# A differential-attention layer on one Trainium2 core: scores by products over 64 rows, three a map, in place of products over 128 rows, four a pair

## The chip, the core and the metric

The kernel runs on one core of one Trainium2 chip. Five engines work side by side, each on its own list of instructions in a fixed order: TensorE (PE) multiplies, VectorE (DVE), ScalarE (ACT) and GpSimd (POOL) do elementwise work, and SyncE (SP) issues the DMAs. They wait for one another through semaphores. TensorE reads its operands from SBUF and writes into eight banks of PSUM; the weights of a product are loaded by an operation of their own, which the profile lists as PEld. The metric is the device time of one execution in microseconds.

## The reference

One layer takes 2048 latent tokens and 128 context tokens of width 1024 through a normalisation, one input projection (queries, keys, values and the three inputs of a short convolution), attention beside convolution, an output projection, and a feed-forward block. The part that matters here is the attention. Each of the four heads has two maps with queries and keys of 64 numbers each; the two softmaxes are subtracted with a learned weight before they meet the values:

```python
s = jnp.einsum('bqhmd,bkhmd->bhmqk', qblk.astype(jnp.float32), kf) * ATTN_SCALE
p = jax.nn.softmax(s, axis=-1)
a = p[:, :, 0] - lam * p[:, :, 1]
return jnp.einsum('bhqk,bkhe->bqhe', a, vf)
```

Latent queries read 2176 keys (2048 latent and 128 cached ones), context queries their own 128. All is held to float32 accuracy.

## The kernel before

**Numbers in two parts.** TensorE takes its operands in a float32 form that it rounds (F32R). So `split` (lines 79 to 82) writes every operand as a rounded part and a remainder: ScalarE copies (L81), VectorE subtracts (L82). A product of two such numbers is then three products: high by high, high by low, low by high.

**Stages.** From 0 to 408 us the input projection and the split queries, keys and values are made. Queries and keys are turned by `stack` (L241) and go to DRAM (`qd`, `kd`, `kpd`). From 408 to about 1370 us lies the attention stage, to 1554 the rest of the output projection, and behind it the feed-forward block, first `psg` (L956 to L959), then `psy` (L1085 to L1087).

**Scores before.** A head vector has 64 numbers, and TensorE has 128 rows to sum over. The kernel lays the high part of a map's key in rows 0 to 63 and its low part in rows 64 to 127, one tile `km[m]` a map. The query tile `qt` has the high part of the query twice, once in each half of the rows, and the low part twice. Two products over 128 rows then give all four combinations, high and low query with the whole key, the fourth (low by low) without being asked for. A block of 128 queries against 2176 keys is done in five pieces of 436 or 432 columns (`KC`), each into one of three PSUM banks (`pss`, tile `s`):

```python
for s in range(2):
    mm = T.matmul(ps[:, :n], qt[:, s, m, t * P:(t + 1) * P], km[m][:, k0:k0 + n], start=(s == 0), stop=(s == 1))
```

VectorE takes each piece out of its bank into `e` with the running maximum (L505). After five pieces it reduces the maxima to `nm` (L509), ScalarE takes the exponential with its sum (L510), and after the second map VectorE forms the weights `r` and `wt` (L513 to L516). GpSimd (L519, L520) and VectorE (L521) share the addition of the second map to the first.

**Values and the filler.** The values of one piece of work (`values`, L526) are computed behind the scores of the next: transposes of `e` on TensorE (L546), a split into `ath` and `atl`, and three products with the values (L537 to L539). Between the scores TensorE gets products of the convolution's inputs (L617 to L619) and, later, of the output projection (L724 to L726). After each eviction `pump` (L781) adds a fixed credit of columns and issues such products, ordered behind the last score product that is in the list `marks`.

**What sets the order.** A scheduler places each engine's instructions when the program is built, by priorities, buffers that come free, and its own estimate of time. On the chip the order of each engine is fixed. The five `e` buffers and one more, the three score banks and the lists on SP are the resources around the change.

Of the kernel before, what the change touches and what calls it, by code (L numbers as in the profile page):

```python
# [8 lines left out]
F32 = mybir.dt.float32  # L9
F32R = mybir.dt.float32r  # L10
BF16 = mybir.dt.bfloat16
AF = mybir.ActivationFunctionType
ALU = mybir.AluOpType
AX = mybir.AxisListType
# [3 lines left out]
P = 128  # L18
# [5 lines left out]
NH = 4  # L24
# [3 lines left out]
SCALE = 0.125  # L28
# [12 lines left out]
def layer(ctx, tc, x_prompt, x_sample, cache_k, cache_v, cond, w_ada, b_ada, gcol,  # L41
# [3 lines left out]
    V, S, G, T = nc.vector, nc.scalar, nc.gpsimd, nc.tensor  # L45

    const = ctx.enter_context(tc.tile_pool(name="const", bufs=1))
    dram = ctx.enter_context(tc.tile_pool(name="dram", bufs=1, space=DRAM))
# [3 lines left out]
    identr = const.tile([P, P], F32R, name="identr")  # L52
# [7 lines left out]
    ud = [dram.tile([2, P, KT, 256], F32, name=f"ud{i}") for i in range(9)]  # L60
    kd = [dram.tile([NH, 2, P, w], F32, name=f"kd{w}") for w in (1792, 384)]
    kpd = dram.tile([NH, 2, P, P], F32, name="kpd")
    qd = [dram.tile([NH, 2, 64, 2, 256], F32, name=f"qd{i}") for i in range(9)]
    vd = dram.tile([18, P, NH, 256], F32, name="vd")
    mixh = [dram.tile([NH, 2, P, 256], F32, name=f"mixh{i}") for i in range(9)]
    mixc = dram.tile([4, 2, P, NALL], F32, name="mixc")
# [3 lines left out]
    def dma(out, in_):  # L70

        out, in_ = (x.bitcast(F32) if x.dtype == F32R else x for x in (out, in_))
        with tc.issue_after(behind[0]) if behind else ExitStack():
            return nc.sync.dma_start(out, in_).ins
# [4 lines left out]
    def split(h, l, src, eng=None):  # L79

        S.copy(h, src)  # L81
        (eng or V).tensor_tensor(l, src, h.bitcast(F32), op=ALU.subtract)  # L82
# [20 lines left out]
    def pool(name, **kw):  # L103
        st = ExitStack()
        return st, st.enter_context(tc.tile_pool(name=name, reuse_waits="tile", **{"bufs": 1, **kw}))
# [135 lines left out]
    def stack(st_list, dst, flip):  # L241

        n = len(st_list)
        for a in range(4):
            tp = psk.tile([P, 512], F32, tag="psk", name="tp")
            tv = tp.rearrange("p (m t) -> p m t", m=2)
            for m in range(2):
                for i, st in enumerate(st_list):
                    T.transpose(tp.bitcast(F32R)[:, m * 256 + i * P:m * 256 + (i + 1) * P],
                                st[:, 2 * a + m, :], identr)  # L250
            o = p1b.tile([P, 2, 256], F32R, tag="sto", name="sto", bufs=2)
            if a % 2 == flip:
                S.copy(o[:, :, :n * P], tv[:, :, :n * P])
            else:
                V.tensor_copy(o[:, :, :n * P], tv[:, :, :n * P])
            dst(a, o, n * P)

    def heads_split(src):

        st = p1b.tile([P, 8, P], F32R, tag="st", name="st", bufs=3)  # L260
        sv = src.rearrange("p (m d) -> p m d", m=8)
        split(st[:, :, 0:64], st[:, :, 64:128], sv)
        return st

    def v_split(src, kt):
# [10 lines left out]

    def q_store(i):
        def f(a, o, n):
            for s in range(2):
                dma(qd[i][a, s, :, :, :n], o[s * 64:(s + 1) * 64, :, :n])  # L280
        return f

    def kp_store(a, o, n):
# [17 lines left out]
    def qkv_out(pq, gi, i, j, rt, sts):  # L301
        if gi == 8 and j > 0:
            so = p1b.tile([P, 512], F32, tag="t1", name="so", bufs=2)
            V.tensor_copy(so, pq)
            dma(state_k if j == 1 else state_v, so)
        if j == 2:
            v_split(pq, 2 * gi + i if gi < 8 else 17)
        else:
            sts.append(heads_split(pq if gi == 8 else rotated(pq, rt, i)))
# [33 lines left out]
    x_pb, p1b = pool("p1b", side="left")  # L343
# [39 lines left out]
    def cached():  # L383
        ck = p1b.tile([P, 512], F32, tag="t1", name="ck", bufs=2)
        dma(ck, cache_k)
        stack([heads_split(ck)], k_store(NLAT), 0)
        cv = p1b.tile([P, 512], F32, tag="t1", name="cv", bufs=2)
        dma(cv, cache_v)
        v_split(cv, 16)
# [11 lines left out]
        bcx_weights(0)  # L401

    def load_q(h, i, w):
        qt = pk.tile([P, 2, 2, 256], F32R, tag="qt", name="qt", bufs=2)
        src = qd[i][h, :, :, :, :w].rearrange("s d m t -> d s m t")
        for s in range(2):
            for r in range(2):
                dma(qt[r * 64:(r + 1) * 64, s, :, :w], src[:, s])
        return qt

    def load_keys(h):
        km = []
        for m in range(2):
            kt_ = pk.tile([P, NALL], F32R, tag="km", name="km", bufs=3)
            dma(kt_[:, :1792], kd[0][h, m])
            dma(kt_[:, 1792:], kd[1][h, m])
            km.append(kt_)
        kp = pk.tile([P, 2, P], F32R, tag="kp", name="kp")
        dma(kp, kpd[h].rearrange("m p t -> p m t"))
        return km, kp  # L420

    wb = {}
# [49 lines left out]
    x_pa, pa = pool("pa", side="left")  # L472
    x_fu, pf = pool("pfu", side="right")
    x_pss, pss = pool("pss", space=PSUM, bufs=3, side="left")
# [6 lines left out]
    def e_tile():  # L481

        ecount[0] += 1
        if x_fu is not None and ecount[0] % 6 == 0:
            return pf.tile([P, NALL], F32, tag="e", name="e")
        return pa.tile([P, NALL], F32, tag="e", name="e", bufs=5)

    def softmaxes(qt, nq, km, kcs):

        nk = sum(n for _, n in kcs)  # L490
        sm = pa.tile([P, 2, 2], F32, tag="sm", name="sm", bufs=3)
        r = pa.tile([P, 2, 2], F32, tag="r", name="r", bufs=3)
        out = []
        for t in range(nq):
            e = []
            for m in range(2):
                et = e_tile()
                mx = pa.tile([P, 5], F32, tag="mx", name="mx", bufs=4)
                for ci, (k0, n) in enumerate(kcs):
                    ps = pss.tile([P, 512], F32, tag="s", name="s")  # L500
                    for s in range(2):
                        mm = T.matmul(ps[:, :n], qt[:, s, m, t * P:(t + 1) * P], km[m][:, k0:k0 + n],  # L502
                                      start=(s == 0), stop=(s == 1))
                        marks.append(mm.ins)
                    V.tensor_scalar(et[:, k0:k0 + n], ps[:, :n], SCALE, None, op0=ALU.mult, op1=ALU.max,  # L505
                                    accum_out=mx[:, ci:ci + 1])
                    pump()
                nm = pa.tile([P, 1], F32, tag="nm", name="nm", bufs=4)
                V.tensor_reduce(nm, mx[:, :len(kcs)], axis=AX.X, op=ALU.max, negate=True)  # L509
                S.activation(et[:, :nk], et[:, :nk], AF.Exp, bias=nm, scale=1.0, accum_out=sm[:, t, m:m + 1])  # L510
                e.append(et)

            V.reciprocal(r[:, t, :], sm[:, t, :])  # L513
            wt = pa.tile([P, 1], F32, tag="wt", name="wt", bufs=3)
            V.tensor_scalar(wt, r[:, t, 1:2], neglam, sm[:, t, 0:1], op0=ALU.mult, op1=ALU.mult)
            V.tensor_scalar(wt, wt, 1e30, -1e30, op0=ALU.min, op1=ALU.max)  # L516
            cut = nk - (POOLW if nk > 128 else 0)
            if cut < nk:
                G.tensor_scalar(e[1][:, cut:nk], e[1][:, cut:nk], wt, 1.0, op0=ALU.mult, op1=ALU.mult)  # L519
                G.tensor_tensor(e[0][:, cut:nk], e[0][:, cut:nk], e[1][:, cut:nk], op=ALU.add)  # L520
            V.scalar_tensor_tensor(e[0][:, :cut], e[1][:, :cut], wt, e[0][:, :cut],  # L521
                                   op0=ALU.mult, op1=ALU.add)
            out.append(e[0])
        return out, r
# [256 lines left out]
    def pump():  # L781

        nonlocal credit
        credit += RATE[x_fu is None]
        while credit > 0:
            with tc.issue_after(marks[-1]) if marks else ExitStack():
                c = next(todo)
            if not c:
                credit = 0.0
                break  # L790
            credit -= c
# [4 lines left out]
    marks = []  # L796
    for n, (h, i) in enumerate(work):
        if i == 0:
            qt = hb.pop("q") if n == 0 else load_q(h, 0, 256)
            km, kp = hb.pop("k") if n == 0 else load_keys(h)  # L800
            vts = load_values(h)
        lat = i < 8
        if i > 0:
            qt = load_q(h, i, 256 if lat else 128)
        if lat:
            ar = softmaxes(qt, 2, km, KC)
        else:
            ar = softmaxes(qt, 1, [kp[:, 0, :], kp[:, 1, :]], ((0, 128),))
        if pending:
            values(*pending)  # L810
        pending = (h, i, ar, vts if lat else vts[17:], 17 if lat else 1)
        ready = max(0, n - 28)
# [71 lines left out]
    start = done  # L884
# [182 lines left out]
    for gn, (c, g) in enumerate(groups):  # L1067
        tiles = seqs[c][3 * g:3 * g + 3]
        w = len(tiles) * P
# [88 lines left out]
```

## Time and profile before

| What | Value |
|---|---|
| Median of three runs | 3085.41 us (3083.14 to 3085.58) |
| The profiled execution | 3085.89 us, span 3084.1 us |
| TensorE busy, over the span | 2914.8 us (95%), granted clock 0.984 |
| VectorE, ScalarE, GpSimd busy | 2082.6 us, 1348.7 us, 1242.9 us |
| Attention stage, 408 to 1370 us: TensorE, VectorE, ScalarE, GpSimd busy | 918.44, 756.61, 571.44, 475.31 us of 962 |
| Score products (L502) and their evictions (L505) | 1296 and 648 |

A busy time is the union of an engine's records. Matmul records overlap: a record lasts longer than the distance to the next start, so the cost of a product is read from the starts in the timeline.

### The profile page before, as it was taken

Reading aid. Unit: us, or ns where it says so; the run is one execution under the profiler, and the core shown is the slowest. Engines: PE = TensorE matmul, PEld = TensorE weight load, DVE = VectorE, ACT = ScalarE, POOL = GpSimd, SP = SyncE. Lnnn points to the kernel's source line nnn. Section 1 sums busy time; section 2 is a strip of 40 time slices with the busy share of each in tenths; the row PEclk is TensorE's granted clock in tenths of the full one; section 3 lists DMA queues with packets and bytes.
Section 4 is the critical chain, followed back from the end, with each engine's and each line's share of the span. In section 5 each row is a group of like instructions: output and inputs, shape, how many; then the busy total and the mean of one; then the engine's idle time right before and its main releaser. Section 6 shows DMA issues by size and latency. Waiting matters only on the chain.

```text
span 3084.1 us, 47310 instructions
## 1 busy us (share of the span) xinstructions
PE 2914.8 (95%) x16921; PEld 2653.6 (86%) x16921; DVE 2082.6 (68%) x4158; ACT 1348.7 (44%) x2383; POOL 1242.9 (40%) x1114
## 2 busy tenths in 40 slices
PE   4899989999999999999999989999999999999998
PEld 3778879998999999988888888999999998788886
DVE  7999568787788887764477775776665554554443
ACT  3323236666565665653344433333333333444432
POOL 7313135554545544532256654554544540111110
PEclk8999999999999999999999999999999999999999
DMA  7777564453454444457645465444632325766663
GB/s 249 249 246 246 171 196 123 136 183 113 136 166 127 139 150 132 119 164 223 183 136 156 150 195 193 145 148 134 238 137 97 102 99 193 239 223 219 219 216 120
DMA packets 351180, 525.25 MB, mean 170 GB/s; under 512 B 33089, under 2 KB 264673, under 8 KB 349153
## 3 DMA queue, kind: packets, MB, share of 16 engines
q1 hardware_dynamic: 350944, 522.23, 52.8%
q8 instruction: 133, 2.18, 0.3%
q14 instruction: 103, 0.84, 0.1%
HBM read 393.79 MB, written 128.34 MB: 169 GB/s over the span
## 4 chain that ended last, share of the span: by engine, by line
PE 65%; DVE 12%; DMA 9%; issue 7%; POOL 4%; ACT 2%; SPq 1%; POOLq 0%; DVEq 0%; ACTq 0%
PE psg L956 6%; PE s L502 6%; PE psg L959 6%; PE psg L957 6%; PE psy L1087 4%; PE psy L1086 4%; PE psy L1085 4%; PE t L546 3%; DVE wi L82 3%; DMA raw<-in_w_fi 2%; PE pq L239 2%; POOL st L918 2%; PE psx L725 2%; PE psx L726 2%; PE psx L724 2%
## 5 line engine op out<-in xcount | busy, mean ns | idle before, releaser
L956 PE MATMUL psg<-u,wi 128*128 128x384 f32 (+1 forms) x1848 | 615.6, 334 | 47.2 <-ACT wi L81 21.1
L957 PE MATMUL psg<-u,wi 128*128 128x384 f32 (+1 forms) x1848 | 606.1, 328 | 0.0
L959 PE MATMUL psg<-u,wi 128*128 128x384 f32 (+1 forms) x1848 | 590.6, 330 | 6.0 <-DVE wi L82 6.0
L505 DVE TENSOR_SCALAR_CACHE_REDUCE e<-s 128x436 f32<-128x436 f32 (+2 forms) x648 | 373.8, 600 | 90.0 <-PE s L502 73.4
L956 PEld LDWEIGHTS psg<-u,wi 128*128 128x128 f32 x1848 | 350.0, 189 | 65.7 <-ACT wi L81 29.6
L502 PE MATMUL s<-km,qt 128*128 128x436 f32 (+1 forms) x1280 | 345.7, 374 | 12.1 <-DVE e L505 9.1
L959 PEld LDWEIGHTS psg<-u,wi 128*128 128x128 f32 x1848 | 347.7, 190 | 10.8 <-DVE wi L82 10.3
L957 PEld LDWEIGHTS psg<-u,wi 128*128 128x128 f32 x1848 | 350.4, 190 | 0.1
L82 DVE TENSOR_TENSOR wo<-rawo,wo 128x1024 fp32r<-128x1024 f32 x132 | 167.0, 1265 | 248.4 <-ACT wo L81 243.7
L82 DVE TENSOR_TENSOR wi<-st,wi 128x512 fp32r<-128x512 f32 x264 | 235.2, 895 | 127.6 <-ACT wi L81 126.1
L510 ACT ACTIVATE e<-e,nm 128x2176 f32<-128x2176 f32 (+1 forms) x136 | 274.0, 2015 | 78.4 <-DVE nm L509 77.7
L81 ACT CAST wi<-st 128x512 fp32r<-128x512 f32 x264 | 163.0, 620 | 323.8 <-POOL st L918 166.2
L1087 PE MATMUL psy<-wo,hhl 128*128 128x512 f32 x748 | 285.8, 391 | 1.8 <-DVE hhl L82 1.8
L1086 PE MATMUL psy<-wo,hhl 128*128 128x512 f32 x748 | 286.3, 390 | 0.9 <-DVE wo L82 0.9
L1085 PE MATMUL psy<-wo,hhl 128*128 128x512 f32 x748 | 285.8, 390 | 0.0
L81 ACT CAST wo<-rawo 128x1024 fp32r<-128x1024 f32 x132 | 139.2, 1054 | 296.2 <-PE psy L1087 286.4
L502 PEld LDWEIGHTS s<-km,qt 128*128 128x128 f32 x1280 | 211.0, 192 | 24.4 <-DVE e L505 15.9
L82 DVE TENSOR_TENSOR atl<-t,ath 128x512 fp32r<-128x512 f32 (+2 forms) x292 | 187.1, 650 | 34.7 <-ACT ath L81 33.9
L81 ACT CAST ath<-t 128x512 fp32r<-128x512 f32 (+2 forms) x292 | 157.2, 554 | 116.2 <-PE t L546 107.6
L918 POOL TENSOR_TENSOR st<-raw,st 128x512 f32<-128x512 f32 x66 | 103.0, 1561 | 231.1 <-DVE wi L82 231.1
L1058 POOL TENSOR_TENSOR rr<-rr,mhalf 128x1 f32<-128x1 f32 x17 | 13.1, 779 | 450.4 <-DVE rr L1057 450.4
L82 DVE TENSOR_TENSOR wi<-raw,wi 128x512 fp32r<-128x512 f32 x198 | 176.6, 892 | 15.7 <-ACT wi L81 15.7
(264 smaller groups left out, 7092.6 us busy)
## 6 DMA issues: line engine op xcount, KB each, us to landing
raw<-in_w_fi SPq DMA_DIRECT2D x132, 512.0 KB, 4.1
rawo<-in_w_fo SPq DMA_DIRECT2D x132, 512.0 KB, 3.4
fu<-ud SPq DMA_DIRECT2D x256, 256.0 KB, 4.7
raw<-in_w_ada SPq DMA_DIRECT2D x48, 512.0 KB, 5.3
u2d<-hl SPq DMA_DIRECT2D x42, 512.0 KB, 3.7
u<-u2d SPq DMA_DIRECT2D x14, 1536.0 KB, 9.4
hr<-hid SPq DMA_DIRECT2D x110, 192.0 KB, 3.5
hid<-hid SPq DMA_DIRECT2D x88, 192.0 KB, 2.1
```

The source lines that it names most:

```text
L81: S.copy(h, src)
L82: (eng or V).tensor_tensor(l, src, h.bitcast(F32), op=ALU.subtract)
L502: mm = T.matmul(ps[:, :n], qt[:, s, m, t * P:(t + 1) * P], km[m][:, k0:k0 + n], start=(s == 0), stop=(s == 1))
L505: V.tensor_scalar(et[:, k0:k0 + n], ps[:, :n], SCALE, None, op0=ALU.mult, op1=ALU.max, accum_out=mx[:, ci:ci + 1])
L510: S.activation(et[:, :nk], et[:, :nk], AF.Exp, bias=nm, scale=1.0, accum_out=sm[:, t, m:m + 1])
L918: G.tensor_tensor(t, x, y, op=op)
L956: T.matmul(ps[:, :n], h[:, ks], u[:, 0, kt, :n], start=start and kt == 0, stop=False, skip_group_check=not start)
L957: T.matmul(ps[:, :n], h[:, ks], u[:, 1, kt, :n], start=False, stop=False, skip_group_check=not start)
L959: T.matmul(ps[:, :n], l[:, ks], u[:, 0, kt, :n], start=False, stop=stop and kt == 3, skip_group_check=not start)
L1085: T.matmul(banks[i][:, b, :], hh, woh_[:, bs], start=(f == 0), stop=False)
L1086: T.matmul(banks[i][:, b, :], hh, wol_[:, bs], start=False, stop=False)
L1087: T.matmul(banks[i][:, b, :], hl, woh_[:, bs], start=False, stop=(f == NF - 1))
```

## The change

Queries and keys are laid out by part instead of by map. A head's vector of 128 numbers now holds map 0 in rows 0 to 63 and map 1 in rows 64 to 127; `km[0]` and the first half of `qt` are the high parts of both maps, `km[1]` and the second half the low parts. `heads_split` and `stack` write this layout, with the same number of transposes and copies. A query tile is stored by one DMA instead of two and loaded by one instead of four, without copies of itself. The scores of a piece for the two maps are written into two banks by six products over 64 rows, three a map, written in the source in turn: map 0, map 1, map 0 and so on. The product of the two low parts is left out. The maxima and exponentials of both maps follow after the pieces of both, and both `e` tiles are taken ahead of the first piece. The three banks, the five pieces and the credit of `pump` are unchanged.

```diff
-    qd = [dram.tile([NH, 2, 64, 2, 256], F32, name=f"qd{i}") for i in range(9)]
+    qd = [dram.tile([NH, P, 2, 256], F32, name=f"qd{i}") for i in range(9)]
@@ stack
-            for m in range(2):
+            for s in range(2):
                 for i, st in enumerate(st_list):
-                    T.transpose(tp.bitcast(F32R)[:, m * 256 + i * P:m * 256 + (i + 1) * P],
-                                st[:, 2 * a + m, :], identr)
+                    T.transpose(tp.bitcast(F32R)[:, s * 256 + i * P:s * 256 + (i + 1) * P],
+                                st[:, a, s, :], identr)
@@ heads_split
-        st = p1b.tile([P, 8, P], F32R, tag="st", name="st", bufs=3)
-        sv = src.rearrange("p (m d) -> p m d", m=8)
-        split(st[:, :, 0:64], st[:, :, 64:128], sv)
+        st = p1b.tile([P, NH, 2, P], F32R, tag="st", name="st", bufs=3)
+        sv = src.rearrange("p (h d) -> p h d", h=NH)
+        split(st[:, :, 0, :], st[:, :, 1, :], sv)
@@ q_store
-            for s in range(2):
-                dma(qd[i][a, s, :, :, :n], o[s * 64:(s + 1) * 64, :, :n])
+            dma(qd[i][a, :, :, :n], o[:, :, :n])
@@ load_q
-        qt = pk.tile([P, 2, 2, 256], F32R, tag="qt", name="qt", bufs=2)
-        src = qd[i][h, :, :, :, :w].rearrange("s d m t -> d s m t")
-        for s in range(2):
-            for r in range(2):
-                dma(qt[r * 64:(r + 1) * 64, s, :, :w], src[:, s])
+        qt = pk.tile([P, 2, 512], F32R, tag="qt", name="qt", bufs=2)
+        dma(qt[:, :, :w], qd[i][h, :, :, :w])
@@ softmaxes
-            e = []
-            for m in range(2):
-                et = e_tile()
-                mx = pa.tile([P, 5], F32, tag="mx", name="mx", bufs=4)
-                for ci, (k0, n) in enumerate(kcs):
-                    ps = pss.tile([P, 512], F32, tag="s", name="s")
-                    for s in range(2):
-                        mm = T.matmul(ps[:, :n], qt[:, s, m, t * P:(t + 1) * P], km[m][:, k0:k0 + n],
-                                      start=(s == 0), stop=(s == 1))
-                        marks.append(mm.ins)
-                    V.tensor_scalar(et[:, k0:k0 + n], ps[:, :n], SCALE, None, op0=ALU.mult, op1=ALU.max,
-                                    accum_out=mx[:, ci:ci + 1])
-                    pump()
+            e = [e_tile() for m in range(2)]
+            mx = [pa.tile([P, 5], F32, tag="mx", name="mx", bufs=4) for m in range(2)]
+            for ci, (k0, n) in enumerate(kcs):
+                ps = [pss.tile([P, 512], F32, tag="s", name="s") for m in range(2)]
+                for x, (sq, sk) in enumerate(((0, 0), (0, 1), (1, 0))):
+                    for m in range(2):
+                        ms = slice(64 * m, 64 * m + 64)
+                        mm = T.matmul(ps[m][:, :n], qt[ms, sq, t * P:(t + 1) * P], km[sk][ms, k0:k0 + n],
+                                      start=(x == 0), stop=(x == 2))
+                        marks.append(mm.ins)
+                for m in range(2):
+                    V.tensor_scalar(e[m][:, k0:k0 + n], ps[m][:, :n], SCALE, None, op0=ALU.mult, op1=ALU.max,
+                                    accum_out=mx[m][:, ci:ci + 1])
+                    pump()
+            for m in range(2):
                 nm = pa.tile([P, 1], F32, tag="nm", name="nm", bufs=4)
...
```

The scheduler places the new products itself, and what it makes of the order in the source can be listed.

TensorE's list before, in the attention stage: `s` is a score bank, `km` the keys of one map, `fb` and `fc` banks of the filler, `o` the values' bank, `t` a transpose.

```order
L539 MATMUL o_5410<-atl_5490,vv_3739 128x256
L502 MATMUL s_5386<-km_3500,qt_5212 128x436 x2
L617 MATMUL fb_5381<-fu_4835,bh_3525 128x256
L618 MATMUL fb_5381<-fu_4836,bh_3525 128x256
L619 MATMUL fb_5381<-fu_4835,bl_3526 128x256
L617 MATMUL fb_5381<-fu_4835,bh_3525 128x256
L618 MATMUL fb_5381<-fu_4836,bh_3525 128x256
L619 MATMUL fb_5381<-fu_4835,bl_3526 128x256
L502 MATMUL s_5396<-km_3500,qt_5212 128x432 x2
```

The same list in the changed program, at the like place: `km_3462` holds the high parts of both maps' keys, `km_3465` the low parts; the banks `s_5782` and `s_5783` belong to map 0 and map 1 of one piece, and so do `s_5798` and `s_5799` of the next.

```order
L499 MATMUL s_5782<-km_3462,qt_5667 128x436
L499 MATMUL s_5782<-km_3465,qt_5667 128x436
L499 MATMUL s_5782<-km_3462,qt_5667 128x436
L536 MATMUL o_5865<-ath_5927,vv_3696 128x256
L537 MATMUL o_5865<-atl_5928,vv_3696 128x256
L499 MATMUL s_5783<-km_3462,qt_5667 128x436
L499 MATMUL s_5783<-km_3465,qt_5667 128x436
L499 MATMUL s_5783<-km_3462,qt_5667 128x436
L615 MATMUL fc_5635<-fu_5268,bh_3480 128x256
```

Where two products over 128 rows stood for a piece of one map, three over 64 rows stand now, and the two maps of a piece stand one behind the other, here with products over 128 rows between them. Over the whole program there are 1944 score products in 509 unbroken stretches: 366 of the stretches are three products of one map, 70 are three of map 0 and then three of map 1, and 22 are six in turn as the source has them. Neighbours of different maps inside a stretch number 292.

VectorE's list before, from the maximum of map 0 of one block to the weights: `nm` are the maxima, `r` and `wt` the weights.

```order
L509 TENSOR_REDUCE nm<-mx 128x1
L505 TENSOR_SCALAR e,mx<-s 128x436 x2
L82 TENSOR_TENSOR atl<-t,ath 128x512
L505 TENSOR_SCALAR e,mx<-s 128x436 x2
L82 TENSOR_TENSOR atl<-t,ath 128x512
L505 TENSOR_SCALAR e,mx<-s 128x432
L638 TENSOR_TENSOR z<-cs__6561,fx 128x256
L638 TENSOR_TENSOR z<-cs__6561,fx 128x128
L509 TENSOR_REDUCE nm<-mx 128x1
L82 TENSOR_TENSOR bl<-braw,bh 128x512
L513 RECIPROCAL r<-sm 128x2
```

VectorE's list in the changed program, at the end of a block:

```order
L503 TENSOR_SCALAR e,mx<-s 128x432
L508 TENSOR_REDUCE nm<-mx 128x1
L503 TENSOR_SCALAR e,mx<-s 128x432
L82 TENSOR_TENSOR atl<-t,ath 128x512
L508 TENSOR_REDUCE nm<-mx 128x1
L503 TENSOR_SCALAR e,mx<-s 128x436 x2
L511 RECIPROCAL r<-sm 128x2
L513 TENSOR_SCALAR wt<-r,neglam,sm 128x1
```

The two maxima of a block, which lay five evictions apart, are now one eviction apart, so the two exponentials on ScalarE follow one another directly ahead of the reciprocal that reads both sums.

More of the change, by code (lines that the diff above doesn't have):

```diff
@@ L412, in load_keys @@
         km = []
-        for m in range(2):
+        for s in range(2):
             kt_ = pk.tile([P, NALL], F32R, tag="km", name="km", bufs=3)
-            dma(kt_[:, :1792], kd[0][h, m])
-            dma(kt_[:, 1792:], kd[1][h, m])
+            dma(kt_[:, :1792], kd[0][h, s])
+            dma(kt_[:, 1792:], kd[1][h, s])
             km.append(kt_)
         kp = pk.tile([P, 2, P], F32R, tag="kp", name="kp")
-        dma(kp, kpd[h].rearrange("m p t -> p m t"))
+        dma(kp, kpd[h].rearrange("s p t -> p s t"))
         return km, kp
@@ L494, in softmaxes @@
         for t in range(nq):
-            e = []
-            for m in range(2):
-                et = e_tile()
-                mx = pa.tile([P, 5], F32, tag="mx", name="mx", bufs=4)
-                for ci, (k0, n) in enumerate(kcs):
-                    ps = pss.tile([P, 512], F32, tag="s", name="s")
-                    for s in range(2):
-                        mm = T.matmul(ps[:, :n], qt[:, s, m, t * P:(t + 1) * P], km[m][:, k0:k0 + n],
-                                      start=(s == 0), stop=(s == 1))
-                        marks.append(mm.ins)
-                    V.tensor_scalar(et[:, k0:k0 + n], ps[:, :n], SCALE, None, op0=ALU.mult, op1=ALU.max,
-                                    accum_out=mx[:, ci:ci + 1])
-                    pump()
+            e = [e_tile() for m in range(2)]
[12 more added lines that the diff above has]
+                    pump()
+            for m in range(2):
                 nm = pa.tile([P, 1], F32, tag="nm", name="nm", bufs=4)
-                V.tensor_reduce(nm, mx[:, :len(kcs)], axis=AX.X, op=ALU.max, negate=True)
-                S.activation(et[:, :nk], et[:, :nk], AF.Exp, bias=nm, scale=1.0, accum_out=sm[:, t, m:m + 1])
-                e.append(et)
+                V.tensor_reduce(nm, mx[m][:, :len(kcs)], axis=AX.X, op=ALU.max, negate=True)
+                S.activation(e[m][:, :nk], e[m][:, :nk], AF.Exp, bias=nm, scale=1.0, accum_out=sm[:, t, m:m + 1])
             V.reciprocal(r[:, t, :], sm[:, t, :])
```

## The prediction

> **What bounds the kernel now.** I read the slices of the span first, then the busy times of the attention stage, then who keeps TensorE waiting there, and last the timeline, for what one product costs. The slices of the page (tenths busy, one digit for 77 us) show TensorE full nearly everywhere:
>
> ```profile
> span 3084.1 us, 47310 instructions
> PE   4899989999999999999999989999999999999998
> DVE  7999568787788887764477775776665554554443
> ```
>
> The scores run in one stage. Its window, its score products alone, and the lines of those products:
>
> ```profile
> 408.00:1370.00 962.00, 918.44 (x6583) 876.32 (x6583) 756.61 (x2125) 571.44 (x1004) 475.31 (x565) 0.99 0.48 142
> 408.00:1370.00 962.00, 347.93 (x1296) 213.05 (x1296) 0.99 0.48 142
> L502 PE MATMUL s<-km,qt x1280: 352/361/735, 408.0 to 1336.4; 128*128 128x436 f32 x147, 128*128 128x432 f32 x36
> L502 PE MATMUL s<-kp,qt x16: 223/274/277, 489.7 to 1193.9; 128*128 128x128 f32 x16
> ```
>
> In the first row the columns are TensorE, its weight loads, VectorE, ScalarE and GpSimd: 918 of 962 us against 757, 571 and 475. So TensorE sets the end of this stage. It has 962 - 918 = 44 us without any record, and the waits on it are short:
>
> ```profile
> PE s L502 <- DVE e L505: 9.1, 11, 1.3
> PE fc L617 <- DMA fu<-ud: 7.4, 10, 2.6
> PE t L546 <- DVE nm L509: 4.0, 2, 3.0
> ...
> DVE e L505 <- PE s L502: 73.4, 105, 5.1
> ...
> DVE r L513 <- ACT e L510: 60.8, 38, 3.1
> ...
> PEld s L502 <- DVE e L505: 15.9, 31, 1.5
> ```
>
> Scores wait for a bank that VectorE has yet to empty for 9.1 + 15.9 = 25 us; VectorE itself waits longer for TensorE (73.4) and for exponentials (60.8), which costs nothing as long as the banks come free in time.
>
> A record's length is not its cost, since records overlap. The timeline gives the distance between starts:
>
> ```profile
> 801.03 0.60 PE L546 MATMUL t<-ident,e 128*128 128x128 f32 x4
> 801.38 0.36 PE L539 MATMUL o<-atl,vv 128*128 128x256 f32 x1
> 801.58 0.28 PE L537 MATMUL o<-ath,vv 128*128 128x256 f32 x1
> 801.70 0.28 PE L538 MATMUL o<-ath,vv 128*128 128x256 f32 x1
> ...
> 802.17 0.95 PE L502 MATMUL s<-km,qt 128*128 128x436 f32 x4
> 802.95 0.28 PE L617 MATMUL fb<-fu,bh 128*128 128x256 f32 x1
> ...
> 489.54 0.53 PEld L502 LDWEIGHTS s<-kp,qt 128*128 128x128 f32 x4
> ```
>
> Four score products start at 802.17 and the next product at 802.95: 0.78 / 4 = 0.195 us each. A product of 256 columns costs 0.12 (801.58 to 801.70). The loads of four weight tiles in the last row, the loads of 0.19 overlapping, start (0.53 - 0.19) / 3 = 0.113 us apart, while the products that use them have only 128 columns. So a weight load has a pace of its own, 0.113, and behind 436 columns (0.195) it is hidden.
>
> **The change part by part.**
>
> *Score products.* Before, a piece of both maps is four products over 128 rows; now six over 64. The columns that stream are the same 436, so each is costed at 0.195. The 320 pieces (4 heads, 16 blocks, 5 pieces) go from 1280 to 1920 products: 640 more, 640 x 0.195 = 124.8 us. The context's four heads go from 16 to 24 products of 128 columns, 8 x 0.113 = 0.9 us. If the two halves of the rows never work at once, that is +126 us.
>
> The change is drawn for the two halves to work at once. No row of before has a product over 64 rows, so the gain has to be bounded. The floor is perfect overlap. But it can only happen between neighbours in TensorE's list, and there the scheduler has not kept the alternation: 366 of the 509 stretches are three products of one map alone. I go through the list with one clock for each half: a product starts when its half is free and no earlier than the product ahead of it. Three of one map take three times, three and three take five (the last of one beside the first of the other), six in turn take three. The 1944 products then take the time of 1730, against 1296 before: 434 x 0.195 = +85 us (before: 1296 x 0.195 = 253). If starts also lie at least 0.113 apart, the pace of the weight loads, they take 1818: 522 x 0.195 = +102 us. I take +102, between 85 and 126, because the weight pace is a row of this trace and six loads of 0.113 are more than three streams of 0.195 (0.68 against 0.585).
>
> The Trainium skill speaks for the overlap: "TensorE: Matmul & The Clock Gate", Part 3: Packing small matmuls, states that products in different row groups run concurrently, and gives 3.07 times for four tiles of 32 rows. By that, the extra is the 85 us, and no run here shows it for this number format.
>
> *Changes between 128 and 64 rows.* Each of the 509 stretches is entered from products over 128 rows and left to them: 1018 changes. None is in the trace. The floor is 0. The ceiling from rows: a score record outlasts its pace by 0.365 - 0.195 = 0.17 us (0.95 for four, three of them at 0.195), and if the next may not begin before that tail is out and its weights are not loaded ahead either, a change costs 0.17 + 0.113 = 0.28, in all 288 us. The nearest row is the return from transposes, another kind of work in the same array: the product behind them holds TensorE from 801.38 to 801.58, 0.20, where its like takes 0.12, so 0.08. I take 0.08 for each change: 1018 x 0.08 = +81 us.
>
> *Waits for banks.* Three banks serve pairs, but in the list three products into one bank follow one another as two did, with the same 648 evictions of about 0.6 us. TensorE now needs longer per bank, so the 25 us of waits for evictions shrink; I take them all off, -25, with 0 as the other end.
>
> *Both exponentials together.* ScalarE's exponentials follow each other directly now, and VectorE's reciprocal waits for the second; behind it in VectorE's list stand evictions, and TensorE waits for these.
>
> ```profile
> L510 ACT ACTIVATE e<-e,nm x136: 385/2116/2137, 416.0 to 1339.3; 128x2176 f32<-128x2176 f32 x128, 128x128 f32<-128x128 f32 x8
> ```
>
> At worst VectorE stands 2.1 us longer in each of the 64 blocks, 135 us. It has 962 - 757 = 205 us free, and more in a longer stage, so I take 0; the cover is that slack. If it failed at half of the blocks, TensorE would lose some 32 x 2.1 = 67 us less what the three banks buffer.
>
> *Queries by fewer DMAs.* SP issues one load for four and one store for two:
>
> ```profile
> qt<-qd SPq DMA_DIRECT2D x128, 128.0 KB, 5.3
> qd<-sto SPq DMA_DIRECT2D x64, 128.0 KB, 2.8
> ```
>
> No wait of TensorE names `qt`; the DMA that it waits for is `fu`, 7.4 us in the row above, which queues on SP beside them. Worth between 0 and 7 us; I take 0. Splits, transposes and copies of the first stage keep their number and size: 0.
>
> Sum: 102 + 81 - 25 = +158 us on the span of 3084.1, so 3242; the profiled execution stands 0.5 us over the median of 3085.41 and 1.8 over its own span, so **3243 us**.
>
> **The rivals.**
>
> *Each change drains the array.* The next product waits for the tail of 0.17 us at every change, and the weights are loaded meanwhile: 102 + 1018 x 0.17 - 25 = +250, 3335 us. For it: a record does last that much longer than its pace. Against it: transposes and products follow each other at 0.08. "TensorEngine Tiling (Array Packing)", Key Properties, in the Trainium skill says this: a change of tiling mode drains the engine. No row of before can confirm it, as no mode changes there. 26%.
>
> *Weights of the same half are not loaded behind a running product.* Of the 1944 products, 1944 - 509 - 292 = 1143 follow one of the same half; each would show its load, 1143 x 0.113 = 129 us more: 3243 + 129 = 3372 us. Against it: with 128 rows the loads are hidden, 0.195 apart in the row at 802.17. The Trainium skill's page on the clock gate, in the same Part 3, says that a load overlaps running products only when the row group differs; the row at 802.17 disagrees for 128 rows. 12%.
>
> *Free changes and full overlap.* 85 + 0 - 25 = +60, 3145 us. For it: nothing measured forbids it. Against it: the 0.08 behind transposes. 14%.
>
> *Several passes.* If this number format needs two passes over 64 rows, scores cost 1944 x 0.39 - 253 = +505 and the time is near 3590 us. Nothing speaks for it. 4%.
>
> *Faster: half the rows, shorter products.* If a product over 64 rows cost less than one over 128, the place would be the same score list. The break-even is at 1296 x 0.195 / 1944 = 0.13 us a product, without any charge for changes. The least that the rows allow is the weight pace, 0.113: 1944 x 0.113 - 253 = -33, 3051 us. Against it: cost follows columns (0.12 for 256, 0.195 for 436), which stay. 3%.
>
> *Hidden.* All of the extra falls into TensorE's 44 idle us and the gaps between records: within 0.2%, about 6 us, which is what a measurement here can tell from no change. Even the floor of 85 is twice the 44. 2%.
>
> **How the numbers follow.** The forecast has 39%, the drain 26, the unhidden loads 12, the free changes 14; passes 4, faster 3, hidden 2. The range takes in the first four: 3145 us for the free changes, and 3385 at the upper end, which is 3084 + 126 + 1018 x 0.17 = 3383 (no overlap, drained changes, no wait saved). Outside lie passes, faster, hidden and the sums of several bad terms. Faster by over 0.2%: 3%; within: 2%; slower: 95%.
>
> **What would show it.** Starts of the products over 64 rows about 0.195 us apart inside one map, and closer only where the maps alternate; TensorE's score time in the stage up by 100 to 126 us and its window longer by about 160; the first product behind a stretch holding TensorE some 0.08 longer than its like (0.17 with a drain); the waits of scores for evictions shorter; VectorE's waits for exponentials longer without a wait of TensorE behind them. The forecast is wrong if products of one map start closer than 0.13, if the stage does not get longer, or if stretches cost more than 0.28 at each end.

## The result, and the profile after

The changed kernel takes 3308.08 us (median of four runs, 3300.45 to 3311.61) against 3084.27 us before: 1.0724 times as long, 95% interval 1.071 to 1.0737. That is 224 us more, where 158 were forecast; the time lies inside the range of 3145 to 3385 us.

The head of the page with the busy slices of two engines, then the window of the attention stage (TensorE, its weight loads, VectorE, ScalarE, GpSimd), then the score products' own view:

```profile
span 3309.8 us, 48400 instructions
PE   4999999999999999999999989999999999999998
DVE  8997456666666666565445777567665554554443
```
```profile
400.00:1570.00 1170.00, 1142.89 (x7115) 903.89 (x7114) 751.14 (x2109) 561.75 (x977) 478.71 (x556) 0.98 0.35 105
```
```profile
L499 PE MATMUL s<-km,qt x1920: 348/359/732, 400.5 to 1560.3; 64*128 64x436 f32 x192
```

All of it lies in the attention stage. The scores began at 408.0 and the last started at 1336.4 before, 928 us apart; now 400.5 and 1560.3, 1160 us: 231 us more, of which a start 7.5 us earlier gives some back. TensorE is still the engine that is full (1143 of 1170 us), and its idle time went down, from 44 to 27 us; VectorE's busy share fell because its 751 us are spread over a longer stage. So the time went into TensorE's own work and not into a new wait. Who waits says the same (engine and tile, who releases, us in total, times, longest):

```profile
DVE e L503 <- PE s L499: 231.3, 266, 9.6
...
DVE r L511 <- ACT e L509: 92.4, 33, 4.7
...
PE s L499 <- DVE e L503: 5.5, 9, 1.2
```

VectorE now waits 231 us for scores where it waited 73. Where TensorE's time goes is read from the timeline of TensorE, here a stretch of six products in turn and one of three of map 0:

```profile
906.79 0.28 PE L615 MATMUL fc<-fu,bh 128*128 128x256 f32 x1
906.91 0.28 PE L616 MATMUL fc<-fu,bh 128*128 128x256 f32 x1
907.03 0.28 PE L617 MATMUL fc<-fu,bl 128*128 128x256 f32 x1
907.24 0.86 PE L499 MATMUL s<-km,qt 64*128 64x436 f32 x6
908.03 0.39 PE L615 MATMUL fc<-fu,bh 128*128 128x256 f32 x1
908.25 0.28 PE L616 MATMUL fc<-fu,bh 128*128 128x256 f32 x1
908.37 0.29 PE L617 MATMUL fc<-fu,bl 128*128 128x256 f32 x1
...
908.74 0.28 PE L617 MATMUL fc<-fu,bl 128*128 128x256 f32 x1
908.95 0.86 PE L499 MATMUL s<-km,qt 64*128 64x436 f32 x3
909.74 0.39 PE L535 MATMUL o<-ath,vv 128*128 128x256 f32 x1
909.97 0.28 PE L536 MATMUL o<-ath,vv 128*128 128x256 f32 x1
```

Two things are to be seen. Six products of two maps hold TensorE from 907.24 to 908.03, 0.79 us, and three of one map from 908.95 to 909.74, the same 0.79: the halves do work at once. And each stretch has a price at both ends. The product ahead of it holds TensorE 907.24 - 907.03 = 0.21 us where its like takes 0.12; the stretch itself takes 0.79 where three products of 0.195 take 0.585; the product behind it takes 908.25 - 908.03 = 0.22 in place of 0.12. That is 0.09 + 0.205 + 0.10 = 0.39 us for one stretch, and there are 509.

A third stretch, one of those that stand in the list as three of map 0 and then three of map 1, shows that the order inside a stretch does not matter. Its rows, of the products and then of the weight loads:

```profile
743.20 0.28 PE L617 MATMUL fc<-fu,bl 128*128 128x256 f32 x1
743.40 0.87 PE L499 MATMUL s<-km,qt 64*128 64x436 f32 x6
744.21 0.39 PE L615 MATMUL fc<-fu,bh 128*128 128x256 f32 x1
```
```profile
743.40 0.51 PEld L499 LDWEIGHTS s<-km,qt 64*128 64x128 f32 x6
```

It takes 0.81. Over all stretches of one kind, the median distances from start to start are these (ns; A is a product of map 0, B of map 1; the first number is from the product ahead to the stretch, the last from the product behind to the one after it; behind AAA many are transposes, hence the 167):

```
list      count   ahead | inside the stretch                | behind
AAA         178    209  |  304  198  287                    |  167
BBB         188    206  |  304  198  286                    |  223
AAABBB       70    209  |   10  293   10  186   10  287     |  223
ABABAB       22    209  |    3  300    3  193    3  284     |  223
```

In AAABBB the starts come in pairs 10 ns apart, as they do in ABABAB: map 1's first product did not wait for map 0's third, although it stands behind it in the list. The records confirm it: the two products that close a bank's sum, and so update a semaphore, stand third and sixth in the list, and in 57 of the 70 stretches the records with the updates are the fifth and sixth to start. So the fixed list does not fix the order of the starts.

So counted by halves, 1944 products take the time of 1560 (each stretch as long as its longer half), not of 1818 as forecast: (1560 - 1296) x 0.195 = +52 us. The stretches' ends give 509 x 0.39 = +198 us. Together +250; the measured 224 is 26 less, of which 17 is the idle time that fell from 44 to 27 us.

### The profile page after: what moved, and what is told of

It reads as the page before. It is cut to its first block, busy times and chain, and to the rows that moved or that the text cites. A ratio compares the mean times of both kernels' runs of the same rounds, so it can differ in the third digit from the quotient of the medians.

```text
span 3309.8 us, 48400 instructions
## 1 busy us (share of the span) xinstructions
PE 3160.2 (95%) x17569; PEld 2697.6 (82%) x17569; DVE 2086.0 (63%) x4158; ACT 1353.9 (41%) x2383; POOL 1251.2 (38%) x1114
## 4 chain that ended last, share of the span: by engine, by line
PE 69%; DVE 11%; DMA 7%; issue 6%; POOL 4%; ACT 2%; SPq 0%; POOLq 0%; DVEq 0%; ACTq 0%
PE s L499 11%; PE psg L954 6%; PE psg L957 6%; PE psg L955 6%; PE psy L1085 4%; PE psy L1083 4%; PE psy L1084 4%; PE t L544 4%; PE fc L615 3%; DVE wi L82 2%; PE o L535 2%; PE o L537 2%; DMA raw<-in_w_fi 2%; PE o L536 2%; PE psx L722 2%
## 5 line engine op out<-in xcount | busy, mean ns | idle before, releaser
L499 PE MATMUL s<-km,qt 64*128 64x436 f32 (+1 forms) x1920 | 453.0, 395 | 6.6 <-DVE e L503 5.5
L499 PEld LDWEIGHTS s<-km,qt 64*128 64x128 f32 x1920 | 258.9, 186 | 89.6 <-issue 16.0
L517 POOL TENSOR_SCALAR e<-e,wt 128x960 f32<-128x960 f32 x64 | 99.3, 1552 | 224.4 <-DVE wt L514 180.0
```

What stands on the lines that cost most here:

```text
L499: mm = T.matmul(ps[m][:, :n], qt[ms, sq, t * P:(t + 1) * P], km[sk][ms, k0:k0 + n], start=(x == 0), stop=(x == 2))
```

## The experiments

The theory is the one just read (theory 1 in the expectations): the loss is the price of going from products over 128 rows to products over 64 and back. Its rivals are the order (theory 2: both maps in pairs over three banks, both exponentials in a row) and dearer products (theory 3). All ratios are to the kernel before, timed on the same chip (3083.08 us beside the kernels over all rows, over rows 0 to 63, map by map and with two pairs; 3082.55 beside the paired maps over 128 rows, the kernel with four score banks and the one with one pair).

### The same list, without the change of rows

```diff
-                        mm = T.matmul(ps[m][:, :n], qt[ms, sq, t * P:(t + 1) * P], km[sk][ms, k0:k0 + n],
+                        mm = T.matmul(ps[m][:, :n], qt[:, sq, t * P:(t + 1) * P], km[sk][:, k0:k0 + n],
```

> The changed kernel with its six products a piece over all 128 rows (map 0 and map 1 summed in each, so the scores are not the reference's); same order, 509 stretches, no change between 128 and 64 rows and no overlap. Theory 1 (the time went into the changes: about 0.39 us for each stretch of 64-row products, read from the starts in the changed kernel's timeline): 1944 x 0.195 - 253 = +126, less up to 25 us of saved waits, 3185 to 3210 us. Theory 2 (it went into the order: both maps in pairs over three banks, both exponentials together): 3308 us or more, since the order stays and the overlap is lost. Theory 3 (every product over 64 rows is dearer, about 0.245 instead of 0.195 us, wherever it stands): 3210 us.

Measured: 3189.93 us, 1.0343 (1.0325 to 1.0362). The list has the same 509 stretches and the same count of products. Two rows of its timeline, six products and then four transposes:

```profile
900.75 1.36 PE L499 MATMUL s<-km,qt 128*128 128x436 f32 x6
901.95 0.60 PE L544 MATMUL t<-ident,e 128*128 128x128 f32 x4
```

Six take 1.20 us, 0.20 each, without a price at the ends. This kernel gives up the overlap, worth (1944 - 1560) x 0.195 = 75 us, and the changes, 198 us; it should lie 123 us under the changed kernel, and lies 3308 - 3190 = 118 under it. Theory 2 falls as the main cause, since the order is kept. Theory 3 expects about the same number here and is told apart by the next run.

### The kernel before, over rows 0 to 63 alone

```diff
-                        mm = T.matmul(ps[:, :n], qt[:, s, m, t * P:(t + 1) * P], km[m][:, k0:k0 + n],
+                        mm = T.matmul(ps[:, :n], qt[0:64, s, m, t * P:(t + 1) * P], km[m][0:64, k0:k0 + n],
```

> The kernel before with its two score products a piece reading only rows 0 to 63 (the low part of the keys is left out); as many products as before, before's order, 476 stretches, all of one half, so no overlap. Theory 1: 476 x 0.39 = +186, less up to 25, 3245 to 3270 us. The prediction's price of 0.08 a change: 952 x 0.08 = +76, 3160 us. Theory 2: order as before, 3084 us. Theory 3: 1296 x 0.05 = +65, 3149 us.

Measured: 3225.99 us, 1.0463 (1.0444 to 1.0482): +143 us with not one product more, before's order and no pairing. Its timeline, a stretch of two:

```profile
903.19 0.28 PE L538 MATMUL o<-ath,vv 128*128 128x256 f32 x1
903.31 0.28 PE L539 MATMUL o<-atl,vv 128*128 128x256 f32 x1
903.51 0.65 PE L502 MATMUL s<-km,qt 64*128 64x436 f32 x2
904.10 0.39 PE L617 MATMUL fb<-fu,bh 128*128 128x256 f32 x1
904.32 0.28 PE L618 MATMUL fb<-fu,bh 128*128 128x256 f32 x1
```

Ahead 0.20 in place of 0.12, inside 0.59 in place of 0.39, behind 0.22 in place of 0.12: 0.38 for a stretch of two, as for one of three or six. So the price goes with the stretch and not with the product, and theory 3 falls. The run lies 19 us under theory 1's window, and 66 us above the 3160 that the prediction's price of 0.08 a change gives. TensorE is then busy 1060 of 1072 us, against 918 of 962 before:

```profile
408.00:1480.00 1072.00, 1060.24 (x6408) 841.81 (x6409) 750.23 (x2099) 554.94 (x965) 460.05 (x551) 0.99 0.41 121
```

Of 476 x 0.39 = 186 us, 143 showed in the time: 44 - 12 = 32 of the missing 43 us are idle time that TensorE had before and no longer has.

### Map by map, over 64 rows

```diff
-            e = [e_tile() for m in range(2)]
...
+            for m in range(2):
+                et = e_tile()
...
+                ms = slice(64 * m, 64 * m + 64)
+                for ci, (k0, n) in enumerate(kcs):
+                    ps = pss.tile([P, 512], F32, tag="s", name="s")
+                    for x, (sq, sk) in enumerate(((0, 0), (0, 1), (1, 0))):
...
```

> The changed kernel with the score loop as before, all pieces of map 0, its exponential, then map 1, three products over 64 rows a piece: 503 stretches, nearly all of one half. Theory 1: products take the time of 1828, +104, and 503 x 0.39 = +196: 3084 + 300, less up to 25, 3360 to 3385 us. Theory 2: the pairing is gone and 648 products are added, 3210 us. Theory 3: the number of products is the changed kernel's, 3308 us.

Measured: 3334.46 us, 1.0813 (1.0797 to 1.083), +251 us, 26 under the window. With almost as many stretches as the changed kernel (503 against 509), hardly any overlap and no pairing it is only 26 us slower than that. The overlap that it lacks is (1828 - 1560) x 0.195 = 52 us, so about half of what the overlap brings the changed kernel is missing from the time. Part of that is idle time of TensorE, 27 of 1170 us there and 13 of 1180 here:

```profile
400.00:1580.00 1180.00, 1167.32 (x7032) 933.25 (x7031) 751.02 (x2090) 552.61 (x963) 464.16 (x548) 0.99 0.34 102
```

That it is the pairing of the maps that loses it is argued, not shown.

### The kernel before with paired maps

```diff
-            e = []
-            for m in range(2):
-                et = e_tile()
...
+            e = [e_tile() for m in range(2)]
+            mx = [pa.tile([P, 5], F32, tag="mx", name="mx", bufs=4) for m in range(2)]
+            for ci, (k0, n) in enumerate(kcs):
+                ps = [pss.tile([P, 512], F32, tag="s", name="s") for m in range(2)]
+                for s in range(2):
+                    for m in range(2):
+                        mm = T.matmul(ps[m][:, :n], qt[:, s, m, t * P:(t + 1) * P], km[m][:, k0:k0 + n],
...
```

> The kernel before, with its products over 128 rows as they are, but with the changed kernel's loop: both maps piece by piece in two of the three banks, both exponentials at the end of a block. Theory 1 (the price lies in the change between 128 and 64 rows): none of it is here, 3083 us within 10. Theory 2 (the pairing of the maps over three banks and the two exponentials in a row cost): slower, up to the 224 us of the changed kernel less its 52 us for longer streaming, 3250 us.

Measured: 3151.00 us, 1.0216 (1.0198 to 1.0235), +68 us: theory 1 missed here. Pairing the maps does cost where TensorE has no other work added. TensorE's waits in the stage:

```profile
PE s L501 <- DVE e L505: 15.5, 24, 1.4
PE o L537 <- ACT ath L81: 15.2, 11, 3.6
...
PE tm L584 <- DVE oc L86: 7.8, 5, 2.7
...
DVE r L513 <- ACT e L511: 82.0, 36, 5.0
...
PEld s L501 <- DVE e L505: 29.0, 53, 1.6
```

The waits of scores and their weights for evictions rose from 25 to 44.5 us, that of the values for a split (`ath`) from 2.8 to 15.2, and VectorE's wait for the exponentials from 61 to 82. Which of the pair's parts does it, the banks or the exponentials, was not separated. In the changed kernel TensorE's waits of these kinds are small (scores for evictions 5.5 us, values for the split 0.6); that this is because TensorE is late itself is argued.

### Pairs that stay together, and the banks they need

Two kernels keep the six products of a piece together by taking both banks as one tile: in the first there are two such tiles and one transpose bank, in the second one such tile and three transpose banks. A third, the kernel before with four score banks and one transpose bank, is the first one's control.

```diff
-                ps = [pss.tile([P, 512], F32, tag="s", name="s") for m in range(2)]
+                pp = pss.tile([P, 2, 512], F32, tag="s", name="s")
+                ps = [pp[:, m, :] for m in range(2)]
...
-    x_pss, pss = pool("pss", space=PSUM, bufs=3, side="left")
-    x_pst, pst = pool("pst", space=PSUM, bufs=2, side="right")
+    x_pss, pss = pool("pss", space=PSUM, bufs=2, side="left")
+    x_pst, pst = pool("pst", space=PSUM, bufs=1, side="right")
```

> The changed kernel with the two banks of a piece taken as one tile, two such tiles (four banks; the transposes get one bank instead of two). TensorE's list then has 307 stretches, 250 of them six products in turn. Theory 1: by halves working at once the products take the time of 980, (980 - 1296) x 0.195 = -62, and 307 x 0.39 = +120: about 3142 us plus what the single transpose bank costs. Theory 2: pairs and exponentials as in the changed kernel: 3308 us or more. Theory 3: the number of products is unchanged, 3308 us.

> The kernel before with four score banks and one transpose bank instead of three and two, as the run with four score banks had them; products over 128 rows, map by map. If that run's 3470 us against the 3142 expected came from the single transpose bank, this kernel loses much of the same 328 us: 3250 to 3410 us. If it came from the pairing, this kernel stands at 3083 us.

> The changed kernel with one tile of two banks for a piece, used again when both are emptied, and three transpose banks: 313 stretches, 303 of them six products in turn. Theory 1: products take the time of 972, (972 - 1296) x 0.195 = -63, and 313 x 0.39 = +122; the earlier runs gave 19 to 50 us less than such sums: 3095 to 3143 us, plus waits for the one pair of banks. Theory 2: pairing as in the changed kernel, 3308 us or more.

Measured: two pairs 3470.34 us, 1.1254 (1.1231 to 1.1278); the control 3370.03, 1.0931 (1.0914 to 1.0947); one pair 3369.29, 1.092 (1.0893 to 1.0947). The two kernels with pairs missed their numbers by far, and neither says how the changed kernel would fare with all pairs together. The control alone, which gains a score bank and loses a transpose bank, is 287 us slower; the longest waits of TensorE there are for the split of what it transposed, 109 us against 6 before:

```profile
PE o L537 <- ACT ath L81: 74.8, 152, 4.5
PE t L546 <- DVE atl L82: 34.0, 111, 1.5
```

Against its control, the kernel with two pairs is 100 us slower, where the price of 307 stretches less the overlap of 980 for 1296 gives +58; what the other 42 us are was not followed. With one pair, TensorE waits for the one pair to be emptied:

```profile
PE s L500 <- DVE e L504: 83.6, 122, 3.2
...
PEld s L500 <- DVE e L504: 119.7, 155, 3.4
```

These three kernels differ from the others in one thing more, the granted clock in the stage (the third number from the end; in the rows below, in order, 0.95 in the control and 0.91 with two pairs and with one; the kernel before has 0.99):

```profile
400.00:1640.00 1240.00, 1069.68 (x6671) 940.69 (x6671) 749.02 (x2128) 587.50 (x1013) 486.83 (x567) 0.95 0.39 114
400.00:1720.00 1320.00, 1117.78 (x7190) 880.67 (x7189) 749.49 (x2122) 579.83 (x995) 487.23 (x565) 0.91 0.32 97
400.00:1640.00 1240.00, 1044.68 (x7179) 859.31 (x7176) 752.24 (x2117) 570.89 (x991) 476.73 (x565) 0.91 0.33 101
```

In the control TensorE is idle for 170 us of the window, against 44 before, and busy for 1070 us against 918 with almost as many products (6671 against 6583). How much of the longer busy time the lower clock costs was not separated.

What they do show in their timelines is the best that a pair can be. In the kernel with two pairs:

```profile
902.62 0.28 PE L618 MATMUL fc<-fu,bl 128*128 128x256 f32 x1
902.83 0.86 PE L500 MATMUL s<-km,qt 64*128 64x436 f32 x6
903.62 0.39 PE L616 MATMUL fb<-fu,bh 128*128 128x256 f32 x1
903.85 0.28 PE L617 MATMUL fb<-fu,bh 128*128 128x256 f32 x1
```

From 902.62 to 903.85 the six hold TensorE 1.23 us less the 0.24 of the two products around them: 0.99. The four products over 128 rows that they stand for took 0.78. So even where every pair stays together, a stretch of one piece loses 0.2 us. By the sum it breaks even with two pieces in one stretch (6 x 0.195 + 0.39 = 1.56 = 8 x 0.195), and the 23 such stretches in this kernel bear it out: by their medians 1.39 us from the first start to the product behind, and 0.20 more on the two products beside them, 1.59 where eight products over 128 rows take 8 x 0.198 = 1.58. A gain lies only beyond; three pieces with all their banks open at once need six of the eight. That was not tried.

## Why the prediction was right, and where not

The direction, the place and the kind of cost were right, the sum almost a third too small (158 of 224). That it came so near is in part luck: the score term was 50 us too high and the term for the changes 117 too low, and a right score term alone would have made the forecast worse (+108). The rival with a drained array, at 3335 us, lies nearer to the measured 3308 than the forecast of 3243. By its steps:

- **What bounds.** Right: TensorE sets the end of the stage before and after, and the whole difference lies in that stage.
- **Score products, +102.** The 0.195 us of a product held (198 ns between the second and third of three). The overlap was under-rated: with this pace and both halves at work, the list gives +52. Two assumptions failed. A product of one half does not queue behind the other half's products that stand ahead of it in the list (starts 10 ns apart in AAABBB), and weight loads do not keep 0.113 apart when they go to different halves (six in 0.51 us; the products of a pair start 3 ns apart where the maps alternate). The sign "closer only where the maps alternate" failed with it. The scheduler's undoing of the alternation mattered only where other products stood between the two maps. The cited claim of the Trainium skill ("TensorE: Matmul & The Clock Gate", Part 3: Packing small matmuls), that different row groups run concurrently, agrees with the trace for this number format: six in the time of three.
- **Changes between 128 and 64 rows, +81: the step that failed.** Mis-sized by more than half: 0.195 us a change against 0.08, 1018 x 0.195 = +198. The row chosen as nearest, the return from transposes, was read on one side only. Its four transposes start (0.60 - 0.27) / 3 = 0.11 us apart (0.27 is one record), and with the product behind them they take 801.58 - 801.03 = 0.55 us, where 4 x 0.11 + 0.12 = 0.56: the product that is held 0.08 longer had also started 0.08 early, so that row has no price to give. (The medians of 100 such groups in the stage are 109 ns between transposes, 28 to the product, 203 behind it.) A change between 128 and 64 rows has two parts that do not cancel, some 0.09 on the product before it, which is not followed as early as usual, and some 0.10 on the product behind it, close to the 0.113 of a weight load. Both kinds were in the upper bound of 0.28, the first as a tail of 0.17. The rival with a drained array (0.17 a change, 3335 us) was nearer on this term, and the rule beside it (the Trainium skill, "TensorEngine Tiling (Array Packing)", Key Properties: a change of mode drains the engine) agrees with what the trace shows at each stretch's end. That it is a drain, rather than another cause of the same length, is argued and not shown.
- **Weights of the same half not hidden: refuted.** Inside a stretch of one map the second distance is 198 ns, and in stretches of six of one half (the run over rows 0 to 63) it stays at 196 or 197 to the end. Only the first distance, 304 ns, is longer, and it comes once a stretch; it is counted in the 0.39. The Trainium skill's statement ("TensorE: Matmul & The Clock Gate", Part 3: Packing small matmuls), that loads overlap only with another row group, does not hold in these rows.
- **Waits for banks, -25.** Scores waited 5.5 us for evictions and their weights 14.4 after, 20 in place of 25; so this name of the saving was wrong. The 25 were too many from the start: by the times of the records before, 9 of the weights' 16 us fall into time in which TensorE runs no product, as do the scores' own 9.1, and the other 7 lie behind products that are still running, so the two waits are not to be added. But 26 us less than the other two terms, as measured, did show in the time, and the sums of the two kernels over 64 rows without pairing were 43 and 50 us too high in the same way: TensorE's short waits of all kinds are used up when its own work grows. That the term had the right size is luck.

```profile
L499 PEld LDWEIGHTS s<-km,qt 64*128 64x128 f32 x1920 | 258.9, 186 | 89.6 <-issue 16.0 <-DVE e L503 14.4 <-ACT sto L253 1.0
```

- **Both exponentials together, 0.** VectorE did wait longer, 92 us for 61, and no wait of TensorE of that length stands behind it. It may not have been quite free: between the first and the last score TensorE is idle for 24 us in the changed kernel and 31 in the one over all rows, both with the pairing, and for 12 in each of the two kernels over 64 rows without it. So some 12 to 19 us may be the pairing's; that is argued from four runs. VectorE's slack, the cover named, is in any case no cover by itself: with products over 128 rows, VectorE at 748 of 1020 us and the same loop, 68 us were lost, to the exponentials or to the banks. That TensorE's own delay is the cover, and that the pairing would cost next if it were taken away, is argued.
- **Queries by fewer DMAs, 0 of 0 to 7.** The scores began 7.5 us earlier, at 400.5 and not 408.0, and between 399.3 and 402.6 in all four other kernels with the new layout, between 406.3 and 407.2 in the three others with the old one. On average that is a start 6 us earlier, near the top of the bounds; which of the DMAs did it was not tried.

The hidden rival fell as its own text had it: the price alone, 198 us, is more than four times TensorE's 44 idle us. For the faster one, products over 64 rows were not shorter: 198 ns from the second to the third of a stretch; the same figure rules out the several passes, which needed 390. The free changes had the overlap nearer than the forecast (85 against 52) and failed on the price of the changes.

Of the signs, the score products' own time in the stage rose by 107 us, from 348 to 455, inside the 100 to 126 named, though it is not made up as forecast, less of it being products and more of it the ends of the stretches:

```profile
400.00:1570.00 1170.00, 455.25 (x1944) 260.54 (x1944) 0.98 0.35 105
```

The first product behind a stretch was held some 0.10 us longer than its like, between the 0.08 of the forecast and the 0.17 of the drain.

## What to carry to other kernels

Splitting the rows of TensorE pays by how long one stays in the split: count the unbroken stretches that the scheduler leaves, not the products saved. Here a stretch costs 0.39 us, as much as two products of 436 columns, so a saving of one product's time in four needs more than two pieces a stretch. Before a new operation is priced by its nearest relative in the trace, list every place at which the relative's neighbours stand late or early, on both sides, and add them up.

## What was not expected of the hardware

- The two halves of the rows take their products independently: six products listed as three and three ran as three pairs, starting 10 ns apart, in 0.81 us.
- A change between products over 128 and over 64 rows costs about 0.195 us each way at these sizes, the same for stretches of two, three and six products.
- The kernel before with one transpose bank in place of two, and four score banks in place of three, is 287 us slower, more than the whole change that was studied. The two halves of that edit, and the lower granted clock (0.95 in the stage), were not separated.
